# A two-layer attention trunk: one seven-product block and three operand sums move from one pair of projections to the next

## The chip, the core and the metric

The kernel runs on one core of a Trainium2 chip. The metric is the device time of one execution in microseconds (us). TensorE (PE) multiplies matrices, VectorE (DVE) and ScalarE (ACT) prepare its operands, GpSimd (POOL) and SyncE (SP) issue the transfers. Each engine works through its own queue in the order in which the program was built; semaphores make one wait for another.

## The reference

```python
# x: (1, 256, 2048); D_INNER 4096, 32 heads of 128; layer A, then layer B
h = rms_norm(x, a_norm)
q, k, v, g = split(h @ a_w_in, 4)              # 2048 -> 4 x 4096
o = chunked_relbias_attention(q, k, v, a_rel_bias)
x = x + (o * silu(g)) @ a_w_out                # 4096 -> 2048
h_kv = rms_norm(x, kv_norm)
k_s, v_s = split(h_kv @ kv_w, 2)
cum_logf = cumsum(log_sigmoid(h_kv @ f_w + f_b))
q, g = split(rms_norm(x, b_norm) @ b_w_in, 2)
o = forgetting_attention(q, k_s, v_s, cum_logf)
x = x + (o * silu(g)) @ b_w_out
return rms_norm(x, final_norm)
```

## The kernel before

**Units and items.** A projection is cut into units of 512 output columns; the accumulators of a unit are two tiles, one for each half of the 256 rows (t = 0, 1). A unit is worked off in items: an item is a weight block of 256 input rows (two slabs of 128) by 512 columns, 512 KB, and it is worth 12 matmuls: two slabs, two halves, and three products each, because weights and activations are both split into a high part (`hi`) and a rest (`lo`) and the product of the two rests is left out. ACT writes `hi` (L248, or L243 with a gain), DVE writes `lo` (L249, L244). Four buffers hold splits that PE has not used up (`SPLIT`), six hold raw weights (`RAW`).

**Quads.** For one block of input rows, two neighbouring units make two slabs by two halves by two units, a 2x2 by 2x2 product. `Quad` makes it with seven products in place of eight: 21 matmuls where two items have 24. DVE pays for it. It makes four sums of weight blocks (L300, L301, L311, L312), and there are seven half blocks to split (`quad_hi0` to `quad_hi3` on ACT, `quad_lo` on DVE) where two items have four. `Quad.step` takes the four splits one after the other; the products p1, p5, p6 and p7 are collected over all quads of a pair in four PSUM banks and combined once per pair (L351 to L355), and the combination is added to the accumulators' result (L744, L831). The activations need sums of their own, which `Quads.sum_up` makes for a block: DVE L393 and L396 to L399, ACT L400, DVE L401.

**Order.** `todo` lists all items and quads in the order in which PE uses them. Layer A's input projections (16 groups of two heads, `aqk`, `avg`) come first, then the output projection (`ao`, four units of 16 items in two pairs: ao0 with ao1, ao2 with ao3), then layer B's input projections (16 groups: `bqg` for q and gate, `bkv` for k and v, eight items each), then `bo`. `Quads.order(first, second, n, lead)` makes quads of the first n blocks of a pair and puts `lead` normal items ahead of the first quad and three between two quads. The first pair of ao has 3 quads and 26 items, the second 5 quads and 22 items. Layer B's groups have one quad each (the third place of `bkv`), except the first group, which has none.

**Work beside the items.** `project` advances side work between items: a list such as [4, 1, 0, 1, 5, 1, 1] says after how many items the next step of a generator is issued. Two of them run beside the first pair of ao: `prev`, the attention of layer A's last group (two heads), and `ao_quads.open`, whose five steps make the sums of blocks 0 to 4. The steps of `prev` are: split of the turned q and k (`wide`, `q`), the scores (PE `s1p` and `s0p`, DVE L586 to L590, ACT L592), the softmax factors (`csc`) and the turn of the probabilities (DVE L522 writes `sgY`; 16 transfers L525 from `sgY` to `sgZ`, half on SP, half on POOL), split of `sgZ` (`wide`), the products with v (PE `op`, L552 to L554 and L616), and the output (`oT`, `oAh`, `oAl`). `oAh` and `oAl` of these two heads are the activations of the last block of the ao units. Each finished ao unit is turned into x1T in the same way (`xinY`, `xinZ`, then ACT L151 and DVE L152 write `x1Th` and `x1Tl`); the last unit is turned by PE (`xT`).

**Layer B's first group.** PE works off eight items of `bqg`, then eight of `bkv`; between them stand the turn of ao3, the forget gates' projection (`zp`, `fps`, `cp`, `cT`, with DVE's chain `f_work`), and, in DVE's and ACT's queues, q and gate of the group. After it, `sum_up` has made the sums of x1T's last block for the quads of groups 1 to 15.

The scheduler that builds the queues may move an instruction a little ahead of or behind the place where the code issues it.

Of the kernel before, what the change touches and what calls it, by code (L numbers as in the profile page):

```python
# [12 lines left out]
AF = mybir.ActivationFunctionType  # L13
OP = mybir.AluOpType
# [4 lines left out]
NT = S // P  # L19
# [33 lines left out]
QUADS = 5  # L53
# [4 lines left out]
QUADS_B = (2,)  # L58
# [2 lines left out]
B1_STEPS = {3: 1, 5: 1, 6: 2}  # L61
B2_STEPS = {1: 1}
OLD_B_STEPS = {0: 1, 2: 99}
FORGET_STEPS = {0: 1, 2: 1, 6: 1, 7: 1}


def r32(ap):
# [9 lines left out]
def trunk(ctx, tc, x, x_t, gains, a_w_in, a_rel, a_w_out, kv_w, f_w, f_b, b_w_in, b_w_out, final_norm, out):  # L77
    nc = tc.nc
    pe, act, dve, pool, sp = nc.tensor, nc.scalar, nc.vector, nc.gpsimd, nc.sync
# [34 lines left out]
    GA, GKV, GB = 0, KD, 2 * KD  # L114
# [31 lines left out]
    def finish(side):  # L146
        advance(side, 99)
# [268 lines left out]
    todo = woven + [i for i in whole(qkvg[1]) if i not in woven]  # L416

    a_quads = Quads("a")

    def paired(specs, places):  # L420

        n = len(places)
        quads = [Quad(a_quads, specs, KD // KB - n + i, not i, i == n - 1, -2 * (i > 0)) for i in range(n)]
        todo.extend(whole(specs[0]))
        for i, item in enumerate(whole(specs[1])):
            todo.append(item)
            todo.extend((None, quads[k]) for k in range(n) if places[k] == i)
        return quads

    a_pairs = [paired(qkvg[2 * g:2 * g + 2], QUADS_A) for g in range(1, NG)]  # L430
    ao = [spec(f"ao{u}", a_w_out[u], KI) for u in range(4)]
    ao_quads, bo_quads = Quads("ao"), Quads("bo")
    ao_order = ao_quads.order(ao[0], ao[1], 3, 14) + ao_quads.order(ao[2], ao[3], QUADS, 4)
    todo += ao_order
    for g in range(NG):
        qkvg.append(spec(f"bqg{g}", b_w_in[g], KD, g0=GB, quads=len(QUADS_B) * (g > 0)))
        qkvg.append(spec(f"bkv{g}", kv_w[g], KD, g0=GKV, quads=len(QUADS_B) * (g > 0)))
    bo = [spec(f"bo{u}", b_w_out[u], KI, LATE if u == 3 else 0, KEPT if u == 3 else 0) for u in range(4)]
    todo += whole(qkvg[2 * NG]) + whole(qkvg[2 * NG + 1])
    b_pairs = [paired(qkvg[2 * g:2 * g + 2], QUADS_B) for g in range(NG + 1, 2 * NG)]  # L440
    bo_order = whole(bo[0]) + whole(bo[1])
    bo_order.insert(KI // KB + WAIT, bo_order.pop(KI // KB - 1))
    bo_order += bo_quads.order(bo[2], bo[3], QUADS, 4)
# [2 lines left out]
    order = iter(qkvg)  # L446
# [26 lines left out]
    def unit(lhs):  # L473
        yield from rest(Unit(lhs, next(order)))

    def rest(u):

        for b in range(u.done, u.plain):
            u.step(b)
            yield u.acc  # L480

    def project(lhs, specs, order, begun, closed, sides):


        units = {}

        def get(u):
            if u not in units:
                units[u] = Unit(lhs, specs[u])
            return units[u]  # L490

        for sp_, b in order:
            if sp_:
                us = [int(sp_["name"][-1])]
                get(us[0]).step(b)
            else:
                us = [int(u["name"][-1]) for u in b.specs]
                b.step(lhs, *(get(u) for u in us))
            for u in us:
                begun(u, units[u].left)  # L500
            for side, steps in sides:
                if steps:
                    steps[0] -= 1
                    while steps and steps[0] <= 0:
                        next(side, None)
                        steps.pop(0)
            for u in us:
                if not units[u].left:
                    more = closed(u, units[u].acc)
                    if more:  # L510
                        sides.append(more)
        for side, _ in sides:
            finish(side)
# [15 lines left out]
    def evac_scaled(acc, c0, c1, rs, dst):  # L529
        for t in range(NT):  # L530
            act.activation(dst[:, t], acc[t][:, c0:c1], AF.Copy, scale=rs[:, t:t + 1])
# [108 lines left out]
    def rows(n, name):  # L640
        return att.tile([P, NT, n], F32, name=name, tag="R")
# [71 lines left out]
    oA = Stat("oA", KI)  # L713
# [26 lines left out]
    def add_whole(acc, i):  # L740

        out = [a_quads.comb[:, i * NT + t] for t in range(NT)]
        for t in range(NT):
            dve.tensor_add(out[t], acc[t], out[t])  # L744
        return out
# [30 lines left out]
    for g in range(NG):  # L776
        accs = {}
        if g:
# [4 lines left out]
            def products(quad):  # L783
                quad.step(xT, first, second)
                if quad.last:
                    for t in range(NT):
                        act.activation(a_quads.comb[:, t], a_quads.comb[:, t], AF.Copy, scale=rsA[:, t:t + 1])
                    advance(side, 2)
# [65 lines left out]
                           accum_out=ssq1[:, t, u:u + 1])  # L854
        return more and (more, [8, 7, 1, 1, 1] if u % 2 else [11, 1, 1, 1])

    project(oA, ao, ao_order, ao_begun, ao_closed, [(prev, [4, 1, 0, 1, 5, 1, 1]), (ao_quads.open(oA, QUADS), [3, 1, 1, 2, 26])])
    tot1 = const.tile([P, NT], F32, name="tot1")
    dve.tensor_reduce(tot1, ssq1, axis=AX.X, op=OP.add)
    rsB, halfB = rstd_of(tot1, "b")  # L860
# [73 lines left out]
    def side_b(g, accs):  # L934
        cb = att.tile([P, HG, S], F32, name="cb", tag="tb")
        sp.dma_start(out=cb, in_=bass.AP(tensor=cumd.tensor, offset=cumd.offset + g * HG * S,
                                           ap=[[0, P], [S, HG], [1, S]]))

        def biases():
            d0 = att.tile([P, HG, P], F32, name="d0")  # L940
            for i in range(HG):
                h = g * HG + i
                act.activation(d0[:, i], cb[:, i, :P], AF.Identity, bias=cum[:, 0, h:h + 1], scale=-1.0)
                act.activation(cb[:, i], cb[:, i], AF.Identity, bias=cum[:, 1, h:h + 1], scale=-1.0)
            for ap in (cb[:, :, P:], d0):
                pool.affine_select(out=ap, in_=ap, compare_op=OP.is_ge, fill=NEG, base=0,
                                   pattern=[[0, HG], [-1, P]], channel_multiplier=1)
            return cb, d0

        qk, gs = accs["q"]  # L950
        kv = accs["kv"]
        if g:
            for t in range(NT):
                whole_ = a_quads.comb[:, NT + t]
                dve.scalar_tensor_tensor(qk[:, t, GC:], kv[t][:, :GC], rsB[:, t:t + 1], whole_[:, :GC],
                                         op0=OP.mult, op1=OP.add)
            for t in range(NT):
                whole_ = a_quads.comb[:, NT + t]
                dve.tensor_add(whole_[:, GC:], kv[t][:, GC:], whole_[:, GC:])
            kv = [a_quads.comb[:, NT + t] for t in range(NT)]  # L960
        else:
            evac_scaled(kv, 0, GC, rsB, qk[:, :, GC:])
        rest_of = attention(g, biases, qk, lambda: (v, gs), halfB, oB, HALVES, ("last", "last"), home)
        next(rest_of)
        yield
        v = v_split(kv, GC, rsB)
        yield
        yield from rest_of

    def open_b(accs, g):  # L970
        qk, qg = rows(UN, "qk"), add_whole(accs["qg"], 0) if g else accs["qg"]
        evac_scaled(qg, 0, GC, rsB, qk[:, :, :GC])
        accs["q"] = qk, gate_from(qg, GC, halfB)

# [1 line left out]
    fg = forget()  # L976
    for g in range(NG):
        accs = {}
        if g:
            first, second = (Unit(x1T, next(order)) for _ in range(2))  # L980
            accs["qg"] = drive(rest(first), prev, B1_STEPS, {}, old, OLD_B_STEPS)

            def products():
                b_pairs[g - 1][0].step(x1T, first, second)
                open_b(accs, g)
                for t in range(NT):
                    k = a_quads.comb[:, NT + t, :GC]
                    act.activation(k, k, AF.Copy, scale=rsB[:, t:t + 1])

            accs["kv"] = drive(rest(second), prev, B2_STEPS, {QUADS_B[0]: products})  # L990
        else:
            accs["qg"] = drive(unit(x1T), last[0], {2: 99})
            accs["kv"] = drive(unit(x1T), fg, FORGET_STEPS, {2: lambda: open_b(accs, g)})
            a_quads.sum_up(x1T, KD // KB - 1, sums[:, 0], a_quads.comb)
        old, prev = prev, side_b(g, accs)
        advance(prev)

# [99 lines left out]
```

## Time and profile before

| | |
|---|---|
| median of 3 runs | 1736.14 us (1734.17 to 1737.35) |
| profiled execution | 1732.83 us, span 1731.1 us |
| PE busy | 1710.2 us (99%), 8213 instructions |
| PE weight loads | 1498.4 us (87%) |
| DVE busy | 1561.4 us (90%) |
| ACT busy | 1195.1 us (69%) |
| POOL busy | 301.0 us (17%) |
| HBM read | 351.05 MB, 205 GB/s over the span |
| PE clock | 0.997 of full speed on average |

All times inside an execution are counted from the start of its span. A row of a timeline gives start, duration, engine, line, operation, output<-inputs, shape and count, and in brackets how long the engine had been idle and what ended that. A row of the chain gives start, duration and what the chain of releases ran through. In a row of waits stand the waiting instruction, what released it, the sum, the number of times and the longest.

### The profile page before, as it was taken

The numbers are of one execution on the slowest core, as the hardware profiler recorded it, in microseconds if no ns is written. First come the engines' busy times: TensorE is split into PE (matmuls) and PEld (weight loads), VectorE is DVE, ScalarE is ACT, GpSimd is POOL, SyncE is SP. The second block draws the span as 40 slices with busy tenths as digits, with TensorE's granted clock in tenths as the row PEclk, the third lists the DMA queues.
The fourth block names the chain that finished last, engine by engine and source line by source line (L and its number), as shares of the span: only waits on it lengthen the run. The fifth ranks groups of instructions, "written<-read, shape, count | busy, mean of one in ns | idle before, by whom it ended". The sixth has DMA issues, their size and how long they took to land.

```text
span 1731.1 us, 26983 instructions
## 1 busy us (share of the span) xinstructions
PE 1710.2 (99%) x8213; PEld 1498.4 (87%) x8213; DVE 1561.4 (90%) x2378; ACT 1195.1 (69%) x2115; POOL 301.0 (17%) x623
## 2 busy tenths in 40 slices
PE   9999999999999999899999999999999999999997
PEld 7888888888888888788888888888888888888886
DVE  8799998999999999888978999999999989996887
ACT  7666666666666666555658788778788878775554
POOL 1011111111111111103102222222222222221000
PEclk9999999999999999999999999999999999999999
DMA  8666666776666666566766666666666666667654
GB/s 309 210 228 245 232 233 206 237 240 235 233 225 231 228 237 231 196 232 225 269 217 219 222 234 231 225 232 229 227 231 232 226 226 229 251 233 251 221 195 146
DMA packets 150320, 396.44 MB, mean 229 GB/s; under 512 B 31104, under 2 KB 51872, under 8 KB 150048
## 3 DMA queue, kind: packets, MB, share of 16 engines
q1 hardware_dynamic: 131536, 373.16, 61.7%
q0 software_dynamic: 17920, 20.48, 4.5%
q8 instruction: 66, 1.08, 0.3%
q10 hardware_dynamic: 720, 1.07, 0.2%
q14 instruction: 78, 0.64, 0.1%
HBM read 351.05 MB, written 4.23 MB: 205 GB/s over the span
## 4 chain that ended last, share of the span: by engine, by line
PE 93%; DVE 3%; DMA 1%; ACT 1%; issue 1%; POOL 0%; SPq 0%; ACTq 0%; DVEq 0%
PE bkv_acc L185 17%; PE bqg_acc L185 17%; PE avg_acc L185 14%; PE aqk_acc L185 13%; PE bo_acc L185 8%; PE ao_acc L185 6%; PE p L553 3%; PE p L554 3%; PE p L552 3%; PE op L616 1%; PE aqk_acc L553 1%; PE s0p L576 1%; PE aqk_acc L554 1%; PE aqk_acc L552 1%; DVE quad_lo L308 1%
## 5 line engine op out<-in xcount | busy, mean ns | idle before, releaser
L525 POOL DMA_DIRECT2D sums<-first x256 | 126.1, 500 | 549.8 <-DVE oT L620 262.5
L243 ACT ACTIVATE bqg_hi<-bqg_raw,gain 128x512 fp32r<-128x512 f32 x226 | 149.5, 713 | 85.6 <-issue 24.9
L244 DVE SCALAR_TENSOR_TENSOR bkv_lo<-bkv_raw,gain,bkv_hi 128x512 fp32r<-128x512 f32 x226 | 161.3, 760 | 17.1 <-ACT bkv_hi L243 16.8
L185 PE MATMUL bkv_acc<-bkv_hi,x1Th 128*128 128x512 f32 x452 | 167.5, 382 | 0.0
L185 PE MATMUL bqg_acc<-bqg_hi,x1Th 128*128 128x512 f32 x452 | 167.4, 382 | 0.0
L185 PE MATMUL bqg_acc<-bqg_lo,x1Th 128*128 128x512 f32 x452 | 166.1, 379 | 0.0
L185 PE MATMUL bkv_acc<-bkv_hi,x1Tl 128*128 128x512 f32 x452 | 166.1, 379 | 0.0
L185 PE MATMUL bkv_acc<-bkv_lo,x1Th 128*128 128x512 f32 x452 | 166.1, 379 | 0.0
L185 PE MATMUL bqg_acc<-bqg_hi,x1Tl 128*128 128x512 f32 x452 | 166.1, 379 | 0.0
L243 ACT ACTIVATE bkv_hi<-bkv_raw,gain 128x512 fp32r<-128x512 f32 x226 | 145.1, 711 | 22.4 <-issue 16.0
L244 DVE SCALAR_TENSOR_TENSOR bqg_lo<-bqg_raw,gain,bqg_hi 128x512 fp32r<-128x512 f32 x226 | 156.2, 741 | 4.6 <-ACT bqg_hi L243 4.5
L525 POOL DMA_DIRECT2D sgZ<-sgY x256 | 125.7, 499 | 156.2 <-PE avg_acc L185 66.7
L185 PE MATMUL aqk_acc<-aqk_hi,xTh 128*128 128x512 f32 x392 | 146.5, 387 | 0.1
L185 PE MATMUL aqk_acc<-aqk_lo,xTh 128*128 128x512 f32 x392 | 143.7, 380 | 1.1 <-DVE aqk_lo L249 1.0
L185 PE MATMUL avg_acc<-avg_hi,xTh 128*128 128x512 f32 x392 | 143.4, 379 | 0.0
L185 PE MATMUL avg_acc<-avg_hi,xTl 128*128 128x512 f32 x392 | 143.4, 379 | 0.0
L185 PE MATMUL avg_acc<-avg_lo,xTh 128*128 128x512 f32 x392 | 143.3, 379 | 0.0
L185 PE MATMUL aqk_acc<-aqk_hi,xTl 128*128 128x512 f32 x392 | 143.3, 379 | 0.0
L249 DVE TENSOR_TENSOR avg_lo<-avg_raw,avg_hi 128x1024 fp32r<-128x1024 f32 x97 | 116.1, 1222 | 16.5 <-ACT avg_hi L248 15.8
L248 ACT ACTIVATE aqk_hi<-aqk_raw 128x1024 fp32r<-128x1024 f32 x95 | 99.9, 1052 | 41.1 <-PE avg_acc L185 15.3
L248 ACT ACTIVATE avg_hi<-avg_raw 128x1024 fp32r<-128x1024 f32 x97 | 100.6, 1052 | 30.8 <-issue 18.1
L249 DVE TENSOR_TENSOR aqk_lo<-aqk_raw,aqk_hi 128x1024 fp32r<-128x1024 f32 x95 | 114.2, 1215 | 5.6 <-ACT aqk_hi L248 5.6
(373 smaller groups left out, 4595.8 us busy)
## 6 DMA issues: line engine op xcount, KB each, us to landing
bqg_raw<-in_b_w_in SPq DMA_DIRECT2D x128, 512.0 KB, 5.1
bkv_raw<-in_kv_w SPq DMA_DIRECT2D x128, 512.0 KB, 4.8
avg_raw<-in_a_w_in SPq DMA_DIRECT2D x127, 512.0 KB, 4.3
aqk_raw<-in_a_w_in SPq DMA_DIRECT2D x125, 512.0 KB, 5.3
ao_raw<-in_a_w_out SPq DMA_DIRECT2D x64, 512.0 KB, 4.7
bo_raw<-in_b_w_out SPq DMA_DIRECT2D x64, 512.0 KB, 4.4
sgZ<-sgY SPq DMA_DIRECT2D x256, 40.0 KB, 2.1
sgZ<-sgY POOLq DMA_DIRECT2D x256, 40.0 KB, 1.9
```

The costliest lines, as they stand in the source:

```text
L185: pe.matmul(acc[t], x[:, t * P:(t + 1) * P], w, start=t not in begun, stop=last and i == 2)
L243: self.by_act = act.activation(hi[:, j], raw[:, j], AF.Copy, scale=gk)
L244: self.by_dve = dve.scalar_tensor_tensor(lo[:, j], raw[:, j], gk, r32(hi[:, j]), op0=OP.mult, op1=OP.subtract)
L248: self.by_act = act.activation(hi[:, j], raw[:, j], AF.Copy)
L249: self.by_dve = dve.tensor_sub(lo[:, j], raw[:, j], r32(hi[:, j]))
L308: feed.by_dve = dve.tensor_sub(lo[:, :n], src, r32(hi[:, :n]))
L525: queues[j].dma_start(out=r32(z)[j * SQ:(j + 1) * SQ, i], in_=y[i * SQ:(i + 1) * SQ, j])
L552: pe.matmul(out_, a[0], b[0], start=start, stop=False)
L553: pe.matmul(out_, a[0], b[1], start=False, stop=False)
L554: pe.matmul(out_, a[1], b[0], start=False, stop=stop)
L576: pe.matmul(s0p[:, i], q0[:, i], qkT[:, HG + i, 0], start=True, stop=True)
L616: pe.matmul(op[:, i, 1::NT], v1[:, i * DH:(i + 1) * DH], pT[:, i, NT], start=False, stop=i == HG - 1)
```

## The change

The first pair of ao gets 2 quads in place of 3, with 17 items ahead of the first in place of 14. The sums of blocks 0 to 4 are made after items 8, 11, 30, 34 and 39 of the projection in place of items 3, 4, 5, 7 and 33; the first pair now has 30 pieces (28 items, 2 quads), so the third sum is issued at its end and the last two in the second pair. All steps of `prev` are issued one item later. Layer B's first group is built as the others are: seven items of `bqg`, seven of `bkv`, and a quad after the third place of `bkv`; the sums for it are made after `bqg`'s third item, and the combination is added as in the other groups. The steps of the forget gates come after other items.

```diff
-FORGET_STEPS = {0: 1, 2: 1, 6: 1, 7: 1}
+FORGET_STEPS = {0: 1, 1: 1, 4: 1, 5: 1}
...
-    ao_order = ao_quads.order(ao[0], ao[1], 3, 14) + ao_quads.order(ao[2], ao[3], QUADS, 4)
+    ao_order = ao_quads.order(ao[0], ao[1], 2, 17) + ao_quads.order(ao[2], ao[3], QUADS, 4)
...
-        qkvg.append(spec(f"bqg{g}", b_w_in[g], KD, g0=GB, quads=len(QUADS_B) * (g > 0)))
-        qkvg.append(spec(f"bkv{g}", kv_w[g], KD, g0=GKV, quads=len(QUADS_B) * (g > 0)))
+        qkvg.append(spec(f"bqg{g}", b_w_in[g], KD, g0=GB, quads=len(QUADS_B)))
+        qkvg.append(spec(f"bkv{g}", kv_w[g], KD, g0=GKV, quads=len(QUADS_B)))
...
-    todo += whole(qkvg[2 * NG]) + whole(qkvg[2 * NG + 1])
-    b_pairs = [paired(qkvg[2 * g:2 * g + 2], QUADS_B) for g in range(NG + 1, 2 * NG)]
+    b_pairs = [paired(qkvg[2 * g:2 * g + 2], QUADS_B) for g in range(NG, 2 * NG)]
...
-    project(oA, ao, ao_order, ao_begun, ao_closed, [(prev, [4, 1, 0, 1, 5, 1, 1]), (ao_quads.open(oA, QUADS), [3, 1, 1, 2, 26])])
+    project(oA, ao, ao_order, ao_begun, ao_closed, [(prev, [5, 1, 0, 1, 5, 1, 1]), (ao_quads.open(oA, QUADS), [8, 3, 19, 4, 5])])
...
-        if g:
-            for t in range(NT):
-                whole_ = a_quads.comb[:, NT + t]
-                dve.scalar_tensor_tensor(qk[:, t, GC:], kv[t][:, :GC], rsB[:, t:t + 1], whole_[:, :GC],
-                                         op0=OP.mult, op1=OP.add)
...
-        else:
-            evac_scaled(kv, 0, GC, rsB, qk[:, :, GC:])
+        whole_ = [a_quads.comb[:, NT + t] for t in range(NT)]
+        for t in range(NT):
+            dve.scalar_tensor_tensor(qk[:, t, GC:], kv[t][:, :GC], rsB[:, t:t + 1], whole_[t][:, :GC],
+                                     op0=OP.mult, op1=OP.add)
+        for t in range(NT):
+            dve.tensor_add(whole_[t][:, GC:], kv[t][:, GC:], whole_[t][:, GC:])
...
+        first, second = (Unit(x1T, next(order)) for _ in range(2))
+
+        def sums_b():
+            finish(last[0])
+            a_quads.sum_up(x1T, KD // KB - 1, sums[:, 0], a_quads.comb)
...
-            accs["qg"] = drive(unit(x1T), last[0], {2: 99})
-            accs["kv"] = drive(unit(x1T), fg, FORGET_STEPS, {2: lambda: open_b(accs, g)})
-            a_quads.sum_up(x1T, KD // KB - 1, sums[:, 0], a_quads.comb)
+            accs["qg"] = drive(rest(first), None, {}, {2: sums_b})
+        accs["kv"] = drive(rest(second), prev if g else fg, B2_STEPS if g else FORGET_STEPS, {QUADS_B[0]: products})
```

The first pair of ao has 375 matmuls of items and quads before (26 items, 3 quads) and 378 now (28 items, 2 quads); layer B's first group has 192 before (16 items) and 189 now (14 items, 1 quad). Lines behind L433 have a number one lower in the changed kernel.

**Place 1: DVE's queue in the first pair of ao, from the scores to the turn.** The first fence is before. Ahead of its rows stand the maxima of the scores (L590), the first row of a sum (L393) and an item's `lo`.

```order
L396 TENSOR_TENSOR ao_quad<-ao_quad 128x128
L397 TENSOR_TENSOR ao_quad<-ao_quad 128x128
L398 TENSOR_TENSOR ao_quad<-ao_quad 128x128
L249 TENSOR_TENSOR ao_lo_7330<-ao_raw_7139,ao_hi_7329 128x1024
L399 TENSOR_TENSOR ao_quad<-ao_quad 128x128
L598 RECIPROCAL csc<-sm 128x4
L249 TENSOR_TENSOR ao_lo_7353<-ao_raw_7157,ao_hi_7352 128x1024
L401 TENSOR_TENSOR ao_sums_7275<-ao_quad,ao_sums_7275 128x512
L599 TENSOR_TENSOR csc<-csc,half_a 128x4
L393 TENSOR_TENSOR ao_quad<-oAh_184,oAl_188 128x512
L249 TENSOR_TENSOR ao_lo_7371<-ao_raw_7175,ao_hi_7370 128x1024
L522 STREAM_TRANSPOSE sgY<-sg 128x1280
```

Now, from the maxima (L589 here) to the turn (L521):

```order
L589 TENSOR_REDUCE nm<-sg 128x2 x2
L249 TENSOR_TENSOR ao_lo_7278<-ao_raw_7139,ao_hi_7277 128x1024
L597 RECIPROCAL csc<-sm 128x4
L598 TENSOR_TENSOR csc<-csc,half_a 128x4
L249 TENSOR_TENSOR ao_lo_7322<-ao_raw_7157,ao_hi_7321 128x1024
L393 TENSOR_TENSOR ao_quad<-oAh_184,oAl_188 128x512
L521 STREAM_TRANSPOSE sgY<-sg 128x1280
```

Between the maxima and the turn stood one whole sum, the beginning of another and four items' `lo`; now stand there two items' `lo` and the beginning of a sum.

**Place 2: DVE's queue in the second pair of ao, from the third split of its second quad.** `xinY` is ao1's turn, `x1Tl` ao0's result. Before:

```order
L308 TENSOR_TENSOR quad_lo_8084<-ao_raw_7908,quad_hi_8083 128x512
L522 STREAM_TRANSPOSE xinY<-xin_7819 128x1024
L308 TENSOR_TENSOR quad_lo_8123<-ao_raw_7906,quad_hi_8122 128x1024
L249 TENSOR_TENSOR ao_lo_8135<-ao_raw_7992,ao_hi_8134 128x1024
L249 TENSOR_TENSOR ao_lo_8147<-ao_raw_8004,ao_hi_8146 128x1024
L152 TENSOR_TENSOR x1Tl_7131<-xinZ,x1Th_7129 128x128 x8
L249 TENSOR_TENSOR ao_lo_8156<-ao_raw_8016,ao_hi_8155 128x1024
L300 TENSOR_TENSOR ao_quad<-ao_raw_8027,ao_raw_8025 128x512
```

Now:

```order
L308 TENSOR_TENSOR quad_lo_8071<-ao_raw_7892,quad_hi_8070 128x512
L521 STREAM_TRANSPOSE xinY<-xin_7795 128x1024
L152 TENSOR_TENSOR x1Tl_7131<-xinZ,x1Th_7129 128x128 x8
L308 TENSOR_TENSOR quad_lo_8106<-ao_raw_7890,quad_hi_8105 128x1024
L249 TENSOR_TENSOR ao_lo_8118<-ao_raw_7983,ao_hi_8117 128x1024
L249 TENSOR_TENSOR ao_lo_8130<-ao_raw_7995,ao_hi_8129 128x1024
L249 TENSOR_TENSOR ao_lo_8139<-ao_raw_8007,ao_hi_8138 128x1024
L393 TENSOR_TENSOR ao_quad<-oAh_185,oAl_189 128x512
L300 TENSOR_TENSOR ao_quad<-ao_raw_8018,ao_raw_8016 128x512
```

The eight `x1Tl` now stand ahead of the quad's fourth split, and the sum of block 4 (from L393) has come between this quad and the next.

**Place 3: DVE's queue in layer B's first group, about where the forget gates begin.** `bkv_lo` are items, `quad_lo` the quad's splits, `first` holds its sums of weights, `f_work` is the gates' chain. Before:

```order
L401 TENSOR_TENSOR sums<-comb,sums 128x512
L244 SCALAR_TENSOR_TENSOR bkv_lo_8823<-bkv_raw_8690,gain,bkv_hi_8822 128x512 x2
L244 SCALAR_TENSOR_TENSOR bkv_lo_8843<-bkv_raw_8710,gain,bkv_hi_8842 128x512 x2
L244 SCALAR_TENSOR_TENSOR bkv_lo_8865<-bkv_raw_8730,gain,bkv_hi_8864 128x512 x2
L244 SCALAR_TENSOR_TENSOR bkv_lo_8920<-bkv_raw_8768,gain,bkv_hi_8919 128x512 x2
L648 SCALAR_TENSOR_TENSOR gs<-gs,bqg_acc_8682 128x256
L648 SCALAR_TENSOR_TENSOR gs<-gs,bqg_acc_8683 128x256
L244 SCALAR_TENSOR_TENSOR bkv_lo_8940<-bkv_raw_8788,gain,bkv_hi_8939 128x512 x2
L894 COPY f_work<-fps 128x64
```

Now:

```order
L401 TENSOR_TENSOR sums<-comb,sums 128x512
L244 SCALAR_TENSOR_TENSOR bkv_lo_8823<-bkv_raw_8683,gain,bkv_hi_8822 128x512 x2
L300 TENSOR_TENSOR first_102<-bkv_raw_8705,bqg_raw_8703 128x512
L301 TENSOR_TENSOR first_102<-bkv_raw_8705 128x512
L308 TENSOR_TENSOR quad_lo_8849<-bqg_raw_8703,quad_hi_8848 128x1024
L311 TENSOR_TENSOR bqg_raw_8703<-bkv_raw_8705,first_102 128x512
L312 TENSOR_TENSOR bqg_raw_8703<-bqg_raw_8703 128x512
L308 TENSOR_TENSOR quad_lo_8902<-first_102,quad_hi_8901 128x1024
L893 COPY f_work<-fps 128x64
```

The quad's first two splits and its four sums of weights stand ahead of the gates' chain, where items stood; the items behind the quad follow later in the queue.

More of the change, by code (lines that the diff above doesn't have):

```diff
@@ L951, in side_b @@
         kv = accs["kv"]
-        if g:
-            for t in range(NT):
-                whole_ = a_quads.comb[:, NT + t]
-                dve.scalar_tensor_tensor(qk[:, t, GC:], kv[t][:, :GC], rsB[:, t:t + 1], whole_[:, :GC],
-                                         op0=OP.mult, op1=OP.add)
[L957 to L960, printed above, removed]
-        else:
-            evac_scaled(kv, 0, GC, rsB, qk[:, :, GC:])
+        whole_ = [a_quads.comb[:, NT + t] for t in range(NT)]
[4 more added lines that the diff above has]
+            dve.tensor_add(whole_[t][:, GC:], kv[t][:, GC:], whole_[t][:, GC:])
+        kv = whole_
         rest_of = attention(g, biases, qk, lambda: (v, gs), halfB, oB, HALVES, ("last", "last"), home)
@@ L968, in side_b, with open_b @@
         yield from rest_of
-    def open_b(accs, g):
-        qk, qg = rows(UN, "qk"), add_whole(accs["qg"], 0) if g else accs["qg"]
+    def open_b(accs):
+        qk, qg = rows(UN, "qk"), add_whole(accs["qg"], 0)
         evac_scaled(qg, 0, GC, rsB, qk[:, :, :GC])
@@ L978, in trunk, with products @@
         accs = {}
+        first, second = (Unit(x1T, next(order)) for _ in range(2))
+        def sums_b():
+            finish(last[0])
+            a_quads.sum_up(x1T, KD // KB - 1, sums[:, 0], a_quads.comb)
+        def products():
+            b_pairs[g][0].step(x1T, first, second)
+            open_b(accs)
+            for t in range(NT):
+                k = a_quads.comb[:, NT + t, :GC]
+                act.activation(k, k, AF.Copy, scale=rsB[:, t:t + 1])
         if g:
-            first, second = (Unit(x1T, next(order)) for _ in range(2))
             accs["qg"] = drive(rest(first), prev, B1_STEPS, {}, old, OLD_B_STEPS)
[L983 to L990, printed above, removed]
-        else:
-            accs["qg"] = drive(unit(x1T), last[0], {2: 99})
-            accs["kv"] = drive(unit(x1T), fg, FORGET_STEPS, {2: lambda: open_b(accs, g)})
-            a_quads.sum_up(x1T, KD // KB - 1, sums[:, 0], a_quads.comb)
+        else:
+            accs["qg"] = drive(rest(first), None, {}, {2: sums_b})
+        accs["kv"] = drive(rest(second), prev if g else fg, B2_STEPS if g else FORGET_STEPS, {QUADS_B[0]: products})
         old, prev = prev, side_b(g, accs)
```

## The prediction

> **What bounds the kernel now.** The page's first row comes first.
>
> ```profile
> PE 1710.2 (99%) x8213; PEld 1498.4 (87%) x8213; DVE 1561.4 (90%) x2378; ACT 1195.1 (69%) x2115; POOL 301.0 (17%) x623
> ```
>
> PE is busy for 1710.2 of 1731.1 us. A change can gain only by taking matmuls away or by closing one of PE's gaps, and DVE, at 90%, is the engine that could open new ones. So I read the busy times of the four stretches that the change touches (first pair of ao, second pair, layer B's groups 0 and 1), and one short stretch inside the first.
>
> ```profile
> core 0: us, PE busy (x) PEld busy (x) DVE busy (x) ACT busy (x) POOL busy (x), PEclk, DMA share, GB/s
> 690.30:781.60 91.30, 86.10 (x399) 74.91 (x398) 77.70 (x111) 48.79 (x72) 11.37 (x25) 0.98 0.64 216
> 781.60:862.40 80.80, 80.31 (x371) 69.44 (x370) 73.41 (x99) 48.44 (x71) 16.29 (x35) 1.00 0.72 247
> 862.40:909.60 47.20, 47.20 (x244) 41.50 (x243) 35.09 (x80) 28.56 (x59) 5.34 (x11) 1.00 0.67 217
> 909.60:951.50 41.90, 41.90 (x200) 36.83 (x200) 34.53 (x57) 34.32 (x71) 9.93 (x20) 1.00 0.63 218
> 729.30:733.10 3.80, 3.75 (x15) 3.49 (x16) 2.94 (x6) 1.25 (x2) 0.61 (x3) 0.59 0.70 262
> ```
>
> Only the first pair has a hole of size: 5.2 of 91.3 us without a matmul, and a clock of 0.59 right behind it. The second pair lacks 0.5 us, layer B's groups nothing. PE's waits in the two pairs say for what:
>
> ```profile
> PE op L552 <- ACT wide L544: 4.2, 1, 4.2
> PE s1p L552 <- ACT q L544: 0.5, 1, 0.5
> PE s0p L576 <- DMA ao_raw<-in_a_w_out: 0.5, 1, 0.5
> PE ao_acc L185 <- ACT ao_hi L248: 0.2, 1, 0.2
> PE ao_acc L552 <- ACT quad_hi L306: 0.2, 1, 0.2
> ```
>
> The first three are `prev`'s; the last two stand in the second pair. The chain shows what lies behind the 4.2 us, and what a matmul costs where nothing waits:
>
> ```profile
> 690.02 0.11 PE op L554
> 690.58 12.97 PE ao_acc L185 x60
> ...
> 718.80 1.42 DVE sgY L522
> ...
> 720.77 3.42 POOL sgZ L525 x7
> 724.19 4.16 DMA sgZ<-sgY
> ...
> 862.43 7.77 PE bqg_acc L185 x36
> ```
>
> 36 matmuls in 7.77 us are 0.216 us each, an item's 12 are 2.59 and a quad's 21 are 4.53. From the start of DVE's turn (718.72) to `op` (729.35), both in the timelines below, pass 10.63 us, and none of it is matmul work.
>
> **The first pair, the term that decides.** 375 matmuls at 0.216 are 80.9 us; the 20 of `s1p`, `s0p` and `op` at 0.11 are 2.2, and 0.3 at the window's edge belong to the group before. 91.3 less 83.4 leaves 7.9 us lost: 5.2 in the three waits, the rest mostly behind `op`, where matmuls start 0.43 apart:
>
> ```profile
> 729.35 0.58 PE L552 MATMUL op<-wide,vh 128*128 128x256 f32 x1 [4.25 <-ACT wide L544]
> 729.72 0.64 PE L185 MATMUL ao_acc<-ao_hi,oAl 128*128 128x512 f32 x1
> 730.15 0.63 PE L185 MATMUL ao_acc<-ao_hi,oAh 128*128 128x512 f32 x1
> ```
>
> How much of it comes back depends on when the turn starts. The rows of DVE before it, then two of ACT, the end of the exponentials and the gates that need DVE's factors:
>
> ```profile
> 704.64 0.28 DVE L545 TENSOR_TENSOR q<-sums,q 128x128 fp32r<-128x128 f32 x1
> ...
> 710.51 1.00 DVE L590 TENSOR_REDUCE nm<-sg 128x2 f32<-128x512 f32 x2
> 711.43 0.68 DVE L393 TENSOR_TENSOR ao_quad<-oAh,oAl 128x512 f32<-128x512 f32 x1
> 712.03 1.22 DVE L249 TENSOR_TENSOR ao_lo<-ao_raw,ao_hi 128x1024 fp32r<-128x1024 f32 x1
> ...
> 718.72 1.51 DVE L522 STREAM_TRANSPOSE sgY<-sg 128x1280 f32<-128x1280 f32 x1
> ...
> 712.90 0.19 ACT L592 ACTIVATION_READ_ACCUMULATOR sg<-sg,nm 128x1 f32 x1
> ...
> 717.10 1.28 ACT L603 ACTIVATE sg<-gs,csc 128x128 f32<-128x128 f32 x4 [0.29 <-DVE csc L599]
> ```
>
> By the order, `s1p` stands behind 72 matmuls of the pair in place of 60, `op` behind 156 in place of 146. At 0.216 each `s1p` is wanted at 690.58 + 15.54 = 706.1; its last operand was made at 704.9, so that wait goes (0.5), and `s0p`'s with it (0.5). `op` is wanted at 690.58 + 33.7 + 1.1 (the scores) = 725.4. Then the turn. The scores end at 707.2 to 707.5 (1.1 us of matmuls, and a little between them); three reads of them (the first two beside the last scores, each some 0.4 by what stood between, an estimate) and the maxima (1.0), with no sum's rows between, end at about 709.3. The exponentials ended 1.6 us after the maxima (713.1 against 711.5): 710.9. The gates need 1.3 us behind the factors, which DVE makes at about 711.3: 712.7. On DVE two `lo` of 1.22 and one L393 of 0.68 stand between the maxima and the turn, where 7.2 us passed before. The second of these `lo` is item 11's, whose buffer comes free when PE ends item 7 (690.58 + 18.1 + 1.1 = 709.8), and it needs ACT's split of about 1 us first: it ends at 712.2, and L393 at 712.8. So the turn starts near 713.2, 5.5 us earlier, and `op` can run at 713.2 + 10.6 = 723.8, 1.6 us before it is wanted. I take 0.3 us left over, since ACT and DVE each have other work between the two splits of `sgZ`, and 0.3 for the small gaps that nothing here touches: 7.9 - 0.6 = **-7.3 us**. The ends: all 7.9 gone, or 2.4 us of wait left over if the turn is ready 4 us later than I have it.
>
> The Trainium skill, "TensorE: Matmul & The Clock Gate", section "What's actually happening", says that PE's clock halves after at least one idle window of about 3.4 us and is full again after about as much work. The trace agrees: 4.25 us idle, then 0.59 in the 3.8 us behind it, and no such stretch behind the waits of half a microsecond (the clock over the whole pair is 0.98). By that rule a rest wait of 2.5 us would cost 2.5; by the proportion of this trace (7.9 lost for 5.2 of waits) it would cost 3.8.
>
> One quad becomes two items: 24 matmuls for 21, +0.65 us on PE (3 x 0.216).
>
> **The second pair.** Two of five sums come into it.
>
> ```profile
> L308 DVE TENSOR_TENSOR quad_lo<-ao_raw,quad_hi 128x1024 fp32r<-128x1024 f32 x10 | 12.2, 1221 | 4.9 <-ACT quad_hi L306 4.8
> L300 DVE TENSOR_TENSOR ao_quad<-ao_raw,ao_raw 128x512 f32<-128x512 f32 x5 | 3.4, 684 | 0.0
> L393 DVE TENSOR_TENSOR ao_quad<-oAh,oAl 128x512 f32<-128x512 f32 x1 | 0.7, 685 | 0.0
> L396 DVE TENSOR_TENSOR ao_quad<-ao_quad 128x128 f32<-128x128 f32 x1 | 0.3, 293 | 0.0
> L401 DVE TENSOR_TENSOR ao_sums<-ao_quad,ao_sums 128x512 fp32r<-128x512 f32 x1 | 0.7, 685 | 0.0
> ```
>
> A sum is 0.685 + 4 x 0.293 + 0.685, at most 2.5 us of DVE; two are 5.1. Stretch two has 80.8 - 73.4 = 7.4 idle, of which 4.9 stands ahead of the quads' splits, most of that at one place:
>
> ```profile
> 805.05 1.70 ACT L151 ACTIVATE x1Th<-xinZ 128x128 fp32r<-128x128 f32 x8 [2.65 <-DVE xinY L522]
> 807.73 1.23 DVE L308 TENSOR_TENSOR quad_lo<-ao_raw,quad_hi 128x1024 fp32r<-128x1024 f32 x1 [2.72 <-ACT quad_hi L306]
> ```
>
> The eight `x1Tl` now stand ahead of this split, in the idle 2.7 us, and the sum of block 4 takes their room behind it. PE lacks 0.5 us in this stretch, nearly all in the two waits behind this ACT row. Bounds: +5.1 if both sums lie bare, -0.5 if both gaps go. The row it is nearest to is the idle time, so the sums are covered; I take half of the gaps, **-0.3**.
>
> **Layer B's first group.** 14 items and a quad have 189 matmuls for 192: **-0.65** on PE. Added to DVE: four sums of weights (2.7), splits 3 x 1.22 + 0.68 (4.3), less four rows of `lo` in place of which they stand (3.0); the combination:
>
> ```profile
> L352 DVE TENSOR_TENSOR comb<-comb,p 128x512 f32<-128x512 f32 x1 | 0.7, 681 | 0.0
> L744 DVE TENSOR_TENSOR comb<-bqg_acc,comb 128x512 f32<-128x512 f32 x2 | 1.4, 680 | 0.0
> ```
>
> Four and two of 0.68, with four small additions of 0.4 behind them: 5.7. In all 9.8 us more, on 35.1 of 47.2. But 4.6 of the idle time is a wait for a transfer and can't be filled:
>
> ```profile
> 872.17 1.10 DVE L152 TENSOR_TENSOR x1Tl<-xinZ,x1Th 128x128 fp32r<-128x128 f32 x5 [4.64 <-ACT x1Th L151]
> ...
> 902.06 0.75 DVE L244 SCALAR_TENSOR_TENSOR bqg_lo<-bqg_raw,gain,bqg_hi 128x512 fp32r<-128x512 f32 x1
> ```
>
> 35.1 + 9.8 + 4.6 = 49.5 us against the 46.5 that PE will need: DVE loses 3.0 us of its lead. The lead at the group's end is what the last row shows: DVE splits group 1's first item at 902.06, and PE uses it at 909.6, 7.5 us later. 4.5 stay, and group 1 leaves DVE 7.4 idle. So the cover holds; I take half of the gain back for a short wait at the quad or the gates, **-0.3** (ends -0.65 and +3.0).
>
> **The sum.** +0.65 - 7.3 (first pair) - 0.3 (second) - 0.3 (layer B) = **-7.25 us**: 1732.83 of the profiled execution to 1725.6. That execution lay 3.3 us below the median of the runs shown, so the forecast is the median less the difference: 1736.14 - 7.25 = **1728.9**.
>
> **Rivals.** *The wait only shrinks.* The turn's landing, not DVE, decides when `op` can start:
>
> ```profile
> DMA to landing us min/median/max: 2.9/4.8/5.7
> ```
>
> This is `sgZ`; the last landing took 4.16 in the chain. For: SP and POOL issue the 16 transfers among weight loads, and the margin is 1.6 us. Against: SP's last load ahead of the turn is freed by the `lo` that ends at 712.2. A turn that is ready 4 us later than worked out leaves 2.4 us: 1728.9 + 2.4 = 1731.3. The Trainium skill, "DMA: Bandwidth & Descriptors", section "Issuing engines are not separate DMA queues", says that transfers of all issuers share the same 16 engines; the spread of landings from 2.9 to 5.7 agrees.
>
> *The second pair pays.* If one of the two sums stands bare between two quads, +2.5 and the 0.3 not won: 1731.7. With both, 1734.3. Against: 7.4 us idle.
>
> *Layer B's first group pays.* If DVE's lead at the group's beginning is nil after its 4.6 us wait, the 3.0 us come out on PE: +3.0 and the 0.3 not won, 1732.2. Against: PE is busy for 47.20 of 47.20 with that wait in it.
>
> *DVE becomes the bound, slower than before.* Net DVE work is +9.8 in layer B and 2.4 - 7.0 = -4.6 in the first pair (a quad's splits and sums against two `lo`), +5.2. If DVE sets the pace from the first pair on, the time is 1736.14 + 5.2 = 1741.3. That decides when the 7.5 us lead falls to nothing; by the sum 4.5 stay.
>
> *The wait doesn't move.* If `sgY` waits for something other than the sums, the 7.3 stay lost and the small rest with them: 1736.1. Against: the last thing it needs, the gates' row at 717.10, waited for `csc`, which stood behind a sum and two items in DVE's own queue.
>
> **How the numbers follow.** Chances: forecast 0.55 (range of its own 1726.5 to 1730.5), shrunk wait 0.17, second pair 0.09, layer B 0.10, wait unmoved 0.05, DVE bound 0.04. A measurement of this kernel can tell about 0.2%, 3.5 us: faster is below 1732.6. The first two cases lie below it, and nearly all of the second pair's and layer B's: 0.86 faster; 0.10 same, 0.04 slower. The range goes down to all gains at their ends, -7.9 - 0.5 and the matmuls even = -8.4, 1727.7, less 2.0 for the spread of the runs (1734.17 to 1737.35), 1725.7; up to both sums bare, 1734.3.
>
> **What would show it.** Right: no wait over 1 us at `op`, the turn near 713, PEclk 1.00 over the first pair and its end 7 us earlier; the second pair's two gaps not larger; layer B's group 0 PE-busy to the end, 0.65 shorter, DVE over 44 us busy in it. Wrong: `op` waits for `sgZ` over 2 us, PE waits for `quad_lo` between the second pair's quads, or for `quad_lo` or `bqg_lo` from 885 on.

## The result and the profile after

The changed kernel takes 1725.12 us (median of 4 runs, 1724.69 to 1726.83) against 1735.16 of the kernel before (4 runs, 1733.26 to 1737.35): a ratio of 0.9944, 95% interval 0.9932 to 0.9956. It is faster, as forecast, but by 10.0 us where 7.25 were forecast, and it lies 0.6 us below the range. The profiled execution took 1724.69 us, its span is 1723.0: 8.1 us below the profiled span before, not 10. Two of the 11 executions of experiment 3's kernel, the profiled one among them, took 1982 and 7434 us and are left out of its figures.

The engines' busy times of the page, then the same stretches as in the prediction (first pair, second pair, layer B's groups 0 and 1; columns as there):

```profile
PE 1707.4 (99%) x8213; PEld 1497.4 (87%) x8213; DVE 1565.7 (91%) x2386; ACT 1198.2 (70%) x2118; POOL 300.7 (17%) x623
```

```profile
690.24:774.14 83.90, 83.90 (x402) 73.76 (x400) 69.80 (x93) 46.53 (x68) 14.39 (x32) 1.00 0.72 242
774.14:854.27 80.13, 79.91 (x370) 69.66 (x369) 76.96 (x111) 49.77 (x73) 13.09 (x27) 1.00 0.71 240
854.27:901.68 47.41, 46.96 (x241) 40.73 (x240) 40.39 (x88) 32.23 (x63) 5.48 (x12) 1.00 0.62 198
901.68:943.59 41.91, 41.91 (x201) 36.84 (x200) 37.30 (x63) 34.43 (x70) 10.05 (x20) 1.00 0.69 241
```

In the first pair PE now works for 83.90 of 83.90 us at a clock of 1.00, although it has three matmuls more. The second pair lacks 0.2 us. In layer B's group 0 a hole of 0.45 us is new, and DVE is busy for 40.4 us there, where over 44 were forecast. All of PE's waits from 680 to 915 us are two:

```profile
PE cT L926 <- DVE cum L922: 0.5, 1, 0.5
PE ao_acc L552 <- DVE quad_lo L308: 0.2, 1, 0.2
```

DVE's rows from the maxima to the turn, the chain that was to decide, and PE's `op` behind it:

```profile
707.80 1.00 DVE L589 TENSOR_REDUCE nm<-sg 128x2 f32<-128x512 f32 x2
708.72 1.22 DVE L249 TENSOR_TENSOR ao_lo<-ao_raw,ao_hi 128x1024 fp32r<-128x1024 f32 x1
...
711.36 1.23 DVE L249 TENSOR_TENSOR ao_lo<-ao_raw,ao_hi 128x1024 fp32r<-128x1024 f32 x1 [0.57 <-ACT ao_hi L248]
712.50 0.69 DVE L393 TENSOR_TENSOR ao_quad<-oAh,oAl 128x512 f32<-128x512 f32 x1
713.10 1.51 DVE L521 STREAM_TRANSPOSE sgY<-sg 128x1280 f32<-128x1280 f32 x1
```

```profile
725.11 0.27 PE L551 MATMUL op<-wide,vh 128*128 128x256 f32 x1
```

The turn starts at 713.10 (forecast 713.2). `op` runs at 725.1 with no idle time before it (forecast: wanted at 725.4).

The matmuls' start times give the length of each piece to a few hundredths; "ao" is from its first matmul to layer B's first. Four columns for each kernel are enough to see where executions differ and where they don't:

| us | layer A, to ao | ao | group 0 | groups 1 to 15 | rest |
|---|---|---|---|---|---|
| before | 690.33 | 171.93 (91.12 + 80.82) | 47.08 | 645.70 | 176.04 |
| changed | 690.24 | 164.03 (83.90 + 80.13) | 47.41 | 645.26 | 176.02 |
| difference | -0.1 | -7.9 (-7.2, -0.7) | +0.3 | -0.4 | 0.0 |

### The profile page after: what moved, and what is told of

Same layout as the page of the kernel before. It is cut to its first block, busy times and chain, and to the rows that moved or that the text cites. A ratio compares the mean times of both kernels' runs of the same rounds, so it can differ in the third digit from the quotient of the medians.

```text
span 1723.0 us, 26992 instructions
## 1 busy us (share of the span) xinstructions
PE 1707.4 (99%) x8213; PEld 1497.4 (87%) x8213; DVE 1565.7 (91%) x2386; ACT 1198.2 (70%) x2118; POOL 300.7 (17%) x623
## 3 DMA queue, kind: packets, MB, share of 16 engines
q10 hardware_dynamic: 720, 1.07, 0.2%
## 4 chain that ended last, share of the span: by engine, by line
PE 76%; DVE 4%; DMA 1%; ACT 1%; issue 1%; POOL 0%; ACTq 0%; DVEq 0%
PE bkv_acc L185 16%; PE bqg_acc L185 16%; PE avg_acc L185 8%; PE aqk_acc L185 8%; PE bo_acc L185 8%; PE ao_acc L185 7%; PE p L552 2%; PE p L551 2%; PE p L553 2%; DVE quad_lo L308 1%; PE op L615 1%; PE s0p L575 1%; DMA xinZ<-xinY 1%; PE aqk_acc L552 1%; PE aqk_acc L553 0%
```

## Experiments

Edits are against the kernel before or the changed kernel, as said. Ratios are to runs of the kernel before on the same chip; experiments 2, 3 and 4 share the runs of the first.

**1. The changed kernel again, in five rounds.** No edit.

> The changed kernel once more, in five rounds beside the kernel before. Open is why the medians differ by 10.0 us where the two profiled executions differ by 8.1. Theory A (the executions of the kernel before lie between 1732.8 and 1737.4, and three of them were too few to place its median): the difference of the medians comes out at 8 to 9 us, and the kernel before spreads wider than the changed one, since its wait for the turn varies from run to run. Theory B (the change gains 10 us, and the one profile hides 2 of them): 9.5 to 10.5 us again.

1725.4 us against 1734.35 (15 runs, 1732.59 to 1739.24): 0.9949 (0.9936 to 0.9961), 8.9 us. Theory A's size holds, and the kernel before spreads over 6.6 us (15 runs) where the changed one spreads over 3.1 (5 runs). That its wait for the turn is what varies was not shown by this run. Its profile has ao at 164.03 again, and layer A at 691.65, 1.4 us longer than in the first.

**2. The output projection's part alone.** Against the kernel before:

```diff
-    ao_order = ao_quads.order(ao[0], ao[1], 3, 14) + ...
+    ao_order = ao_quads.order(ao[0], ao[1], 2, 17) + ...
-    [(prev, [4, 1, 0, 1, 5, 1, 1]), (ao_quads.open(oA, QUADS), [3, 1, 1, 2, 26])]
+    [(prev, [5, 1, 0, 1, 5, 1, 1]), (ao_quads.open(oA, QUADS), [8, 3, 19, 4, 5])]
```

> Only the output projection's part (two quads with 17 items ahead, the later steps); layer B's first group as before. If the wait for the turn is all of the gain: no wait at op, the turn near 713.1, and 7.5 to 8.5 us below the kernel before, so within 0.5 us of the changed kernel. If layer B's first group gives 1 us or more of the gain (which would explain a part of the 10 us): 5 to 7 us below the kernel before.

1726.23 us, 0.9954 (0.9942 to 0.9967), 8.1 us below the kernel before and 0.8 above the changed kernel. ao takes 164.03 us, group 0 47.08 as before. The gain is the output projection's.

**3. Layer B's first group alone.** The changed kernel with `order(ao[0], ao[1], 3, 14)` and the steps of before.

> Only layer B's first group with its quad; the output projection as before. If the quad's three matmuls (-0.65 us) are paid back by the wait at cT: within 0.5 us of the kernel before, op's wait of about 4.2 us still there. If the group gains by itself: 1 to 2 us below. If DVE's 9.8 us more come out on PE: 2 to 3 us above.

1734.92 us (9 runs), 0.9998 (0.9988 to 1.0007): no difference. The stretches come from a second run:

> One profile of layer B's part alone: op's wait of 4.2 us is there, the stretch from ao to layer B takes 171.9 us as before, and layer B's group 0 47.4 us (cT's wait stands against the three matmuls), within 0.1 us of the changed kernel's, if it doesn't depend on what the output projection does.

1733.92 us in that one. ao takes 171.93 us, group 0 47.13. PE's waits:

```profile
PE op L551 <- ACT wide L543: 4.2, 1, 4.2
PE s0p L575 <- DMA ao_raw<-in_a_w_out: 0.5, 1, 0.5
PE cT L926 <- DVE cum L922: 0.4, 1, 0.4
PE s1p L551 <- ACT q L543: 0.4, 1, 0.4
PE ao_acc L185 <- ACT ao_hi L248: 0.2, 1, 0.2
PE ao_acc L551 <- ACT quad_hi L306: 0.2, 1, 0.2
```

The waits of before are all there, and `cT`'s new one with them: the quad saves three matmuls (0.65 us) and the group is 0.05 longer than before. It was forecast within 0.1 us of the changed kernel's 47.4; it is 0.3 shorter. `cT`'s wait is 0.4 here as there; what is missing is some 0.25 us that the changed kernel's first profile loses at the quad's `quad_lo`, counted between matmul starts.

**4. The steps alone, with three quads.** The kernel before with these steps, third sum ahead of the third quad:

```diff
-    [(prev, [4, 1, 0, 1, 5, 1, 1]), (ao_quads.open(oA, QUADS), [3, 1, 1, 2, 26])]
+    [(prev, [5, 1, 0, 1, 5, 1, 1]), (ao_quads.open(oA, QUADS), [8, 3, 8, 15, 5])]
```

> The kernel before with its three quads in the first pair and 14 items ahead of the first; only the steps are moved: prev's one item later and the sums after items 8, 11, 19, 34 and 39. Layer B's first group as before. If the order of the steps is the whole cause: the turn near 713, no wait at op, and 0.6 us (three matmuls) below ao_only, so 8 to 9 us below the kernel before. If giving up the third quad is needed: a wait of over 1 us at op or at the quads, and a gain of 6 us or less.

1727.33 us, 0.9956 (0.9942 to 0.9970), 7.0 us below the kernel before, and 1.1 above ao_only where 0.6 below was expected. ao takes 165.78 us, 84.58 and 81.20 in the pairs. PE's waits there, and the two pairs' busy times:

```profile
PE ao_acc L185 <- DVE ao_lo L249: 1.0, 1, 1.0
PE op L616 <- issue: 0.4, 1, 0.4
PE op L553 <- DMA ao_raw<-in_a_w_out: 0.3, 1, 0.3
```

```profile
692.96:777.54 84.58, 83.88 (x398) 73.34 (x397) 75.51 (x105) 48.31 (x71) 11.94 (x25) 1.00 0.69 233
777.54:858.74 81.20, 80.18 (x370) 69.58 (x369) 75.06 (x105) 49.22 (x72) 16.30 (x34) 1.00 0.74 245
```

The turn starts 22.86 us behind ao's first matmul, exactly as in the changed kernel, and the 4.2 us wait is gone. So the steps make the gain. What is left against the changed kernel is 1.75 us (165.78 - 164.03), although this kernel has three matmuls (0.65 us) less. 0.68 of it lies in the first pair, at `op`, where DVE's queue reads:

```profile
725.16 1.22 DVE L308 TENSOR_TENSOR quad_lo<-ao_raw,quad_hi 128x1024 fp32r<-128x1024 f32 x1
...
727.50 0.42 DVE L545 TENSOR_TENSOR wide<-sgZ,wide 128x256 fp32r<-128x256 f32 x1
727.83 0.68 DVE L312 TENSOR_TENSOR ao_raw<-ao_raw 128x512 f32<-128x512 f32 x1
728.43 0.42 DVE L545 TENSOR_TENSOR wide<-sgZ,wide 128x256 fp32r<-128x256 f32 x1
```

Rows of the first quad, which here follows 14 items, stand ahead of and between the two splits of `sgZ` (`wide`). The first of the two waits at `op` ends at 728.90, right behind the second split; what the other one waits for no view names. In the changed kernel the first quad follows 17 items, and its first row (L300, at 728.27) comes behind both splits. The third quad has no part in this: DVE begins its sums of weights at 751.9, and PE has no wait in the first pair after `op`. The other 1.07 us lie in the second pair, where an item's `lo` comes 1.0 us late. There the last two sums are made one piece later than in the changed kernel, since the first pair has 29 pieces and not 30. `prev_later` below, with three quads and only one sum in the second pair, has no such wait (80.83 us). So 1.75 us is the worth of several things at once: one quad less, a first quad three items later, and the last three sums at other places. Two quads behind 14 items, or three behind 17, were not tried.

**5. Each move alone.** The kernel before with only `prev` later, and with only the sums later:

```diff
+    [(prev, [5, 1, 0, 1, 5, 1, 1]), (ao_quads.open(oA, QUADS), [3, 1, 1, 2, 26])]     prev_later
+    [(prev, [4, 1, 0, 1, 5, 1, 1]), (ao_quads.open(oA, QUADS), [8, 3, 8, 15, 5])]     sums_late
```

> The kernel before with prev's steps one item later and nothing else: three quads, sums after items 3, 4, 5, 7 and 33 as before. The stretch from ao's first matmul to layer B's first took 171.9 us before, 164.0 in the changed kernel and 165.8 with both moves and three quads. Theory 1 (each of the two moves alone suffices, since op is wanted 10 matmuls later and fewer items stand between the maxima and the turn): the turn starts 24 to 26 us behind ao's first matmul (28.4 before, 22.9 now), op waits under 1.5 us, the stretch takes 165 to 168 us. Theory 2 (the sums in DVE's queue decide): op waits 2.5 us or more, 169 to 172 us.

> The kernel before with the sums after items 8, 11, 19, 34 and 39 and nothing else: three quads, prev's steps as before. Theory 1 (each move alone suffices): no wait at op, those at s1p and s0p of half a microsecond each stay, the turn starts 20.5 to 22 us behind ao's first matmul, the stretch takes 165.5 to 167.5 us. Theory 3 (op's later place decides, the sums don't matter): op waits 2.5 us or more, 169 to 172 us.

`prev_later`: 1728.46 us, 0.9957 (0.9941 to 0.9974). ao 165.53 us, the turn 26.26 us behind ao's first matmul, and at `op` and `s0p`:

```profile
PE op L616 <- issue: 0.4, 1, 0.4
PE s0p L576 <- issue: 0.3, 1, 0.3
```

`sums_late`: 1729.43 us, 0.9964 (0.9951 to 0.9977). ao 166.09 us, the turn at 22.02, nothing at `op`. `s0p`'s wait is as before, `s1p`'s is shorter, and the late `lo` of experiment 4 is there too (second pair 81.21 us):

```profile
PE ao_acc L185 <- DVE ao_lo L249: 1.0, 1, 1.0
PE s0p L576 <- ACT ao_hi L248: 0.5, 1, 0.5
PE s1p L552 <- ACT q L544: 0.2, 1, 0.2
```

Theory 1 holds: each move alone takes the 4.2 us wait away, and the two together, at 165.78 us, are no better than the first alone. Theories 2 and 3, which each name one of the moves as the cause, fall. With the first, `op` is wanted some 2 us later (10 matmuls) and the turn starts 2.1 us earlier; with the second, the turn starts 6.4 us earlier.

**6. How much room `op` has, and what a wait costs.** The changed kernel with `op` earlier:

```diff
-    [(prev, [5, 1, 0, 1, 5, 1, 1]), ...
+    [(prev, [5, 1, 0, 1, 4, 1, 1]), ...     op_4
+    [(prev, [5, 1, 0, 1, 3, 1, 1]), ...     op_3
```

> The changed kernel with op one item earlier (12 matmuls, 2.6 us). In the changed kernel DVE's last split for op ended 1.2 us before op ran, so a wait of 1.2 to 1.7 us is made at op. Theory C (a wait under 3.4 us leaves the clock alone): the stretch from ao to layer B grows by the wait, 165.2 to 165.9 us in place of 164.0, and matmuls behind op start 0.22 us apart. Theory D (any wait costs half as much again, as 5.2 us of waits cost 7.9 before): 165.9 to 166.6 us.

> The changed kernel with op 22 matmuls earlier (134 in place of 156, 4.7 us). The wait made at op is 3.3 to 4 us, about as long as the one of the kernel before (4.2). Theory C: if it stays under 3.4 us, the stretch grows by the wait alone, 167.3 to 167.5 us; if it is over 3.4 us and holds a whole window of the clock gate, matmuls behind it start 0.43 us apart for 3 to 4 us, and 1.5 us more are lost, 169 to 169.5 us. Theory D: 169 us or more at any length.

`op_4` (1724.62 us, one run) made no wait: ao 164.25 us. DVE's and ACT's splits of `sgZ` come earlier too, ending 32.2 us behind ao's first matmul and not 33.7. What I had read as the end of `op`'s room, the splits' end, was only their place in the queues. `op_3` (1726.96 us, one run) made a wait of 1.4 us, ao 166.25. PE's rows there:

```profile
722.18 0.38 PE L551 MATMUL op<-wide,vh 128*128 128x256 f32 x1 [1.44 <-ACT wide L543]
722.39 0.38 PE L185 MATMUL ao_acc<-ao_hi,oAl 128*128 128x512 f32 x1
722.61 0.38 PE L185 MATMUL ao_acc<-ao_hi,oAh 128*128 128x512 f32 x1
...
723.82 0.68 PE L615 MATMUL op<-sgZ,v 128*128 128x128 f32 x4 [0.28 <-DMA ao_raw<-in_a_w_out]
```

Matmuls behind it start 0.22 us apart, where 0.43 stood behind the 4.25 us wait before. The stretch grew by 2.2 us: counted between matmul starts, 1.6 at the gap, 0.4 at the second, 0.2 as in `op_4`. So waits of this length cost about what they last, and Theory D's half as much again (2.6 us for the 1.7 of idle time in these rows) falls for them. The length at which the clock falls was not reached by this run (a wait of 3.3 to 4 us was expected).

Two more profiles of the kernel before (experiment 8) narrow it: there the wait at `op` was 3.46 and 3.83 us. Behind the 3.83 matmuls start 0.43 us apart at once, as behind the 4.25. Behind the 3.46 they first start 0.22 us apart, and the clock falls 1.5 us later (`before_p1`; the granted clock is the third number from the end of a window's row):

```profile
729.34 0.38 PE L552 MATMUL op<-wide,vh 128*128 128x256 f32 x1 [3.46 <-ACT wide L544]
729.55 0.38 PE L185 MATMUL ao_acc<-ao_hi,oAl 128*128 128x512 f32 x1
```

```profile
729.34:730.80 1.46, 1.37 (x8) 1.12 (x8) 1.46 (x4) 1.21 (x2) 0.07 (x1) 1.00 0.99 396
730.80:734.21 3.41, 3.19 (x10) 2.77 (x11) 2.28 (x4) 0.63 (x1) 1.17 (x3) 0.50 0.36 138
```

So the length lies between 1.4 and 3.46 us here. Why the clock fell so late in this execution stays open. The rule of the Trainium skill that the prediction cites ("TensorE: Matmul & The Clock Gate", "What's actually happening": an idle window of about 3.4 us) agrees with these lengths.

**7. The two gaps that are left.** The changed kernel with:

```diff
-FORGET_STEPS = {0: 1, 1: 1, 4: 1, 5: 1}
+FORGET_STEPS = {0: 1, 1: 1, 4: 1, 6: 1}
-        return more and (more, [8, 7, 1, 1, 1] if u % 2 else [11, 1, 1, 1])
+        return more and (more, [8, 7, 1, 1, 1] if u % 2 else [14 if u == 0 else 11, 1, 1, 1])
```

> The changed kernel with the two gaps that it leaves in the stretches it touches taken aim at: the last step of the forget gates comes one item later (cT 4 matmuls, 0.86 us, later, against a gap of 0.6 to 0.7 us), and x1T's splits of ao0 begin three items later, so that six and not eight of them stand ahead of the quad's fourth split (0.4 us, the size of that gap). If the two waits are what the stretches lose: the second pair takes 79.7 to 79.8 us in place of 80.13, layer B's group 0 46.7 to 46.8 in place of 47.41, 1 us in all; the runs' medians can hardly tell that. If DVE is short there, the waits only move to the next split, and the stretches stay within 0.15 us.

> The changed kernel beside the trimmed one on the same chip. The stretch from ao's first matmul to layer B's first took 164.03 us in two profiles, layer B's group 0 47.41 and 47.35: the same again, to 0.05 us, while layer A's stretch differs by up to 1.5 us. The difference of the medians to the kernel before: 8 to 9 us.

1725.78 us against 1725.73 of the changed kernel on the same chip: nothing gained. Both waits are gone and both stretches keep their length: the second pair 80.11 us (80.12), with a new gap of 0.28 us (between matmul starts) at the next quad's `quad_lo`; group 0 46.65 and group 1 42.25, together 88.9 (88.8 in the changed kernel beside it). DVE is what is short there, and the wait goes to the next split. The changed kernel's median here was 8.4 us below the kernel before (0.9950, 0.9938 to 0.9962).

**8. Is the rest of the difference in layer A?** Two profiles of each kernel in turn.

> The kernel before, one profile more. The stretches the change touches were shorter by 7.6 us, while the medians differ by 8.4 to 9. Layer A's part, whose instructions are the same in both kernels, took 690.3 to 693.0 us in five profiles with the old first group of layer B (mean 692.0) and 690.2 to 691.7 in seven with the new (mean 690.7). If that is chance: 690.2 to 693, no nearer to 692.0 than to 690.7. If the rest of the gain lies there: 691 to 693 in this one and the next.

> The changed kernel, one profile more. If layer A's length is chance: 690.2 to 693 us to ao's first matmul. If it goes with the kernel: 690 to 691.5. From ao's first matmul to layer B's first 164.03 us.

> As the first of these profiles: layer A's part 690.2 to 693 us with no preference if it is chance, 691 to 693 if it goes with the kernel; ao 171.9 us.

> As the second: layer A's part 690.2 to 693 us with no preference if it is chance, 690 to 691.5 if it goes with the kernel; ao 164.03 us.

| us | spans | layer A, to ao | ao | group 0 |
|---|---|---|---|---|
| before, 3 profiles | 1731.1, 1731.5, 1730.8 | 690.33, 691.19, 690.34 | 171.93, 171.73, 171.55 | 47.08 in all |
| changed, 5 profiles | 1723.0, 1725.1, 1723.7, 1725.7, 1724.3 | 690.24, 691.65, 690.43, 692.33, 690.83 | 164.03 in all | 47.41, 47.35, 46.92, 47.30, 46.71 |

By layer A's part it is chance: the changed kernel has the longest and the shortest. The spans' means differ by 6.8 us (1731.1 and 1724.4); in the touched stretches it is 7.6 (ao 171.74 to 164.03, group 0 47.08 to 47.14). The four medians of the kernel before (1735.16, 1734.35, 1734.98, 1734.17) lie above its three profiled executions (1732.83, 1733.21, 1732.54). None of these profiles shows where its longer executions spend the rest, so that stays open. The wait at `op` differs by 0.8 us among the three (3.46 to 4.25), the ao stretch by only 0.4. Of the 33 executions of this kernel whose mean granted clock is on record, six show 0.996, the three longest (1737.9 us and more) among them; the others, and the three profiles, show 0.997 or 0.998. A further 3.4 us at half the rate would make such a difference of 0.001 (an estimate: 1.7 of 1735 us), and so a part of it; no trace of such an execution was taken.

## Why the prediction was right and wrong

In the output projection the mechanism came as argued, down to the turn's start; in layer B the quad gained nothing. Where the numbers failed:

- **First pair, -7.3 + 0.65.** Measured -7.2 (91.12 to 83.90) where -6.65 was forecast. The 7.9 us of loss were right, and all of it came back. Mis-sized was the 0.6 us that I kept: 0.3 for a rest wait at `op`, which op_4 shows to have had at least 2.6 us more room, and 0.3 for small gaps "that nothing here touches", of which none is left.
- **The 10.6 us from the turn to `op`.** I carried it over as fixed. It contained the landings: 2.9 to 5.7 us before, and in the changed kernel

```profile
DMA to landing us min/median/max: 1.8/2.0/2.3
```

  op_4 needed 9.4 us. So the rival of the shrunk wait, which took the landing for the limit, went the other way: a turn that starts earlier landed sooner.
- **Second pair, -0.3.** Measured -0.7 (80.82 to 80.13). The two sums lay in idle time, as argued; both old gaps went, and one of 0.4 us came (counted between matmul starts; at `quad_lo`, behind the `x1Tl` that now stand ahead of it).
- **Layer B, -0.3.** Measured +0.3 in the first profile and +0.06 in the mean of five. The three matmuls are paid back, most of them at `cT`: it waits for `cum`, which in DVE's queue stands behind the new combination and has no idle time before it:

```profile
897.72 0.68 DVE L743 TENSOR_TENSOR comb<-bqg_acc,comb 128x512 f32<-128x512 f32 x1
...
900.31 0.22 DVE L922 COPY cum<-cp 128x64 f32<-128x64 f32 x1
```

  I had named the gates as the place of a wait, but gave it half of the 0.65. Of DVE's 9.8 us more, 5.3 fell into group 0 (35.1 to 40.4) and 2.8 into group 1. They did not come out on PE beyond these waits, so DVE as the bound and the group that pays both fell.
- **The sum and the step that failed.** On the stretches -7.6 (mean of the profiles) stands against -7.25. What missed is the last step, "the forecast is the median less the difference": the median of three runs, 1736.14, was too high a base. Later medians of the same kernel are 1734.2 to 1735.2, so 1 to 2 us of the 3.8 by which the forecast missed are the base. From those medians the same difference gives 1726.9 to 1727.9, against 1725.1 to 1725.7 measured. The 1.2 to 2.8 us that are still missing are the 0.4 of the stretches and the rest of experiment 8, whose cause stays open. From the profiled execution, 1732.83, the sum gave 1725.6; that it is so near is luck in part, since the changed kernel's five profiled executions lie between 1724.7 and 1727.4. The difference of 10.0 us did not come again either: 8.9 and 8.4 followed. The low end of the range was built from the same base and fell 0.6 us short.

Of the cases, the forecast's own came by its mechanism, though below its own range of 1726.5 to 1730.5; no run showed the wait in the second pair, the loss in layer B or DVE as the bound. What the prediction didn't look at is the place of the first quad. It costed the edit as two items for a quad, +0.65 us; with nearly the same steps the kernel with three quads is 1.75 us longer (experiment 4), 0.68 of them where its first quad stands among the splits for `op`.

## What to carry to other kernels

Before a chain of hand-offs that ends in a wait of the busiest engine, list what stands in each queue between its first and last step; moving the consumer later by one item, or taking unrelated work out of the producer's queue, may each be enough, and the second move then adds nothing. A block that saves the busy engine matmuls at the price of another engine's work has to be placed with that engine's queue in view: in experiment 4 one that stood three items earlier put its splits among those of `op`, and PE waited 0.7 us. And measure such an edit by the length of the stretch that it touches (164.03 us five times in five) before the end-to-end time, which moved by 3 us between executions.

## What the runs showed of the hardware

The same 16 transfers of 40 KB landed in 2.9 to 5.7 us when the turn came at 718.7, and in 1.8 to 2.3 when it came at 713.1. With layer B's part alone, where the turn is late again, it was 2.9 to 5.6. In the trace of before SP issued four weight loads of 512 KB between 713.3 and 719.2, just ahead of those transfers; in `prev_later` three, with landings of 1.9 to 3.5 us; in the changed kernel the last one ahead was out 1.7 us before the turn's first. That this is the cause was not tried.

A wait of 1.4 us left PE's clock alone. Waits of 3.46, 3.83 and 4.25 us were each followed by a stretch at a granted clock of 0.50, in which matmuls start 0.43 us apart; by the traces' clock records it lasted 3.41 us in all three. Behind the shortest it began only 1.5 us after matmuls had resumed.
